# RWKV's chunk inverses per head on 64x64 quadrants instead of block-diagonal 128x128 matrices of two heads

## The chip, the core and the metric

One NeuronCore of a Trainium2 chip runs the whole program: TensorE (PE) for matmuls, VectorE (DVE), ScalarE (ACT) and GpSimd (POOL) for the elementwise work, SyncE (SP) and the others' queues for DMA. The metric is the device time of one execution in microseconds; three runs are given by their median, 3457.86 us (3451.37 to 3464.75).

## The reference, cut to what matters

Three blocks follow one another (an attention and retention block, a gated MLP and state space block, and a block with sparse attention and RWKV). The change is in the third block's RWKV part: 512 tokens, 8 heads of 64. For every head a state of 64x64 is carried from token to token:

```python
def _wkv7_step(state, inp):
    r, w, k, v, a, b = inp
    sa = jnp.einsum('bhvk,bhk->bhv', state, a)
    state = state * w[:, :, None, :] + sa[..., None] * b[:, :, None, :] + v[..., None] * k[:, :, None, :]
    return state, jnp.einsum('bhvk,bhk->bhv', state, r)

def rwkv7_time_mix(feats, w0, w2, a0, a2, g2, k_k, k_a, r_k, ln_w, ln_b):
    ...
    kk = heads(k * k_k)
    kk = kk / jnp.maximum(jnp.sqrt(jnp.sum(kk * kk, axis=-1, keepdims=True)), 1e-12)
    k = k * (1.0 + (a - 1.0) * k_a)
    ...
    xs = tuple(z.transpose(1, 0, 2, 3) for z in (rh, heads(decay), kh, vh, -kk, kk * ah))
    _, y = lax.scan(_wkv7_step, state0, xs)
    ...
```

Because each step adds a product of the state with `a` back into the state, a chunk of 64 tokens can be done at once only with the inverse of a triangular 64x64 matrix, (I - L)^-1, where L holds the products of the chunk's `a` and `b`, masked below the diagonal.

## The kernel before

The 8 heads are taken as 4 pairs. A pair fills the 128 partitions: head 0 in rows 0 to 63, head 1 in rows 64 to 127. Each pair has 8 chunks of 64 tokens, and all matrix work on chunks is in fp32.

`rwkv` runs, for each pair t: `raw` (three projections of the block's normed input, TensorE lines L250 to L252 with their weights split on ScalarE and VectorE), `features` (decays, normalised keys, the operands `ar`, `b`, `kt`), `prepare` (per chunk the matrix L and its inverse) and `steps` (the chunks in turn). They overlap by generators: while the 8 steps of pair t run, `prepare` of pair t + 1 advances by a stage per step, and after the fourth step `raw` and `features` of pair t + 2 are issued. During the last pair's steps, the sparse attention's preparation runs instead. The order in which the instructions of each engine stand is then fixed when the program is built, and projections of later blocks are spread between the small matmuls.

In `prepare` the chunks come in two groups u = 0, 1 of four. The steps that the change touches:

- L1705 and L1706 (GpSimd) copy `b` and `kt` into `bbd` and `kbd`, 128x128 matrices per chunk with head 0's 64x64 block in the upper left and head 1's in the lower right; the other blocks are zero from the start.
- L1710 (and L1764 for `kbd`) is the Gram product of this matrix with `ar`, 128 columns per chunk. L1712 (VectorE) masks it into `lt`, again block-diagonal, and L1717 and L1718 form the first `XT` (2x2 blocks and identity).
- `flip` (L1726) transposes `XT` per chunk on TensorE, L1727 copies it to `X`.
- `level(l)` for l = 1 to 5 doubles the diagonal blocks: GpSimd masks `lt` (L1736), L1741 multiplies it with half of X's columns, L1743 (ScalarE) copies the result into `ys`, L1747 multiplies that with half of XT's columns, L1749 (VectorE) adds it to XT, and a flip follows (except after the last).
- In `steps`, L1811 multiplies the inverse `xt` with a right hand side that L1805 copied; L1803, L1810, L1823 and L1826 are the other products of a step, one per head. L1816 and L1829 are VectorE links of the chain from step to step.

All per-chunk matrices of both heads are 128 wide, and half of each is zero:

```python
                    nc.tensor.matmul(g1[:, n].rearrange("p u l -> p (u l)"), bbd[u][:, n], rhs, start=True, stop=True)
                    nc.tensor.transpose(tt[:, n], XT[u][:, n], K.ident)
                        nc.tensor.matmul(y[u][:, n], ls[:, n], half(X[u], 0)[:, n], start=True, stop=True)
                        nc.tensor.matmul(yx[u][:, n], ys[u][:, n], half(XT[u], 1)[:, n], start=True, stop=True)
                nc.tensor.matmul(sa, xt[:, n], rs_, start=True, stop=True)
```

Of the kernel before, what the change touches and what calls it, by code (L numbers as in the profile page):

```python
# [7 lines left out]
def tw(w):  # L8
    """[K, N] -> [N/128, 128, K]: block n holds, for each row within a row block, its row blocks' 128 columns"""
    K, N = w.shape  # L10
    return np.ascontiguousarray(
        w.reshape(K // 128, 128, N // 128, 128).transpose(2, 1, 0, 3)).reshape(N // 128, 128, K)


def tn(w):
    """[K, m] -> [128, K/128 * m]"""
    K, m = w.shape
    return np.ascontiguousarray(w.reshape(K // 128, 128, m).transpose(1, 0, 2)).reshape(128, K // 128 * m)


def il(w, n=2):
    """block order a0 a1 .. b0 b1 .. -> a0 b0 a1 b1 .."""
# [4 lines left out]
class Vec:  # L27
    """per-feature vectors, packed as columns of [128, n]"""
# [14 lines left out]
    def dup(self, name, v):  # L43
        """a [64] vector on both halves"""
# [13 lines left out]
def shape_consts():  # L58
# [10 lines left out]
    half = 64  # L69
# [11 lines left out]
    m = np.zeros((128, 8, 128), f)  # L81
    m[:, 0, :64] = np.arange(64)[None, :] > h[:, None]
    m[:, 0, 64:] = np.arange(64)[None, :] >= h[:, None]
    b = i[:, None] // 64 == i[None, :] // 64
    for l in range(6):
        z = 1 << l
        s_, t_ = h[:, None], h[None, :]
        m[:, 1 + l] = b & (s_ // (2 * z) == t_ // (2 * z)) & (s_ // z % 2 == 0) & (t_ // z % 2 == 1)
    m[:, 7, 0] = i >= 31
# [13 lines left out]
def arrays1(I, vec):  # L103
    """layouts for the first block"""
# [92 lines left out]
class Ctx:  # L197
# [13 lines left out]
    def psum(self, mm, s=0, t=0, o=0):  # L211
        """the banks: for projections, scores, transposes, and sums over several steps"""
# [19 lines left out]
    def wunit(self, src, kc, m=P):  # L232
        """src: DRAM AP [128, kc*m]; gives hi, lo tiles [128, kc, m]."""
# [20 lines left out]
    def ahead(self, key, *args, **kw):  # L254
        """a block whose result is asked for later, by the same key"""
        self.early[key] = self.block(*args, **kw)

    def block(self, srcs, xs, halves, m=P, pss=None, first=True, last=True, key=None, unit=None):
        """srcs: list of (DRAM AP, kc); xs: list over all kc of (hi, lo) APs [128, T].
        halves: list of (start, size) of token columns. Returns psum APs."""  # L260
# [33 lines left out]
    def stacked(self, out, x, s):  # L294
        """rows 64 s .. of x: hi parts in the same rows of out, lo parts in the other half"""
# [5 lines left out]
    def twice(self, hi, lo, x, s):  # L301
        """hi and lo parts of rows 64 s .. of x, each on both halves"""
# [7 lines left out]
    def unstack(self, out, ps):  # L310
        """the two halves of a bank added"""
# [13 lines left out]
    def sq_acc(self, acc, h, first, scale=1.0):  # L325
        """acc += (h * scale)^2"""
# [9 lines left out]
    def rstd(self, acc, halves, eps, name, pool=None, factor=None):  # L336
        """rstd of the columns, times factor if there is one, on all partitions: exp(-ln(mean + eps) / 2)"""
# [31 lines left out]
    def swiglu(self, w_up, w_dn, zs, rs, halves, hid, done):  # L369
        """w_up: DRAM [44, 128, 1024] with blocks a0 b0 a1 b1 ..; w_dn: [8, 128, 22*128]."""  # L370
# [21 lines left out]
    def setup_consts(self, c):  # L392
        """c: DRAM [128, 7, 128]: identity, blocks of 1/64, a quarter of the upper triangle, last row,
        causal mask (0 / -1e30 above), 1/256, 1/512"""
# [23 lines left out]
    def bcast(self, ap):  # L418
        """DRAM AP read by all partitions"""
        return bass.AP(tensor=ap.tensor, offset=ap.offset, ap=[[0, P]] + [list(x) for x in ap.ap])  # L420

    def log1p(self, out, y, s, q):
        """ln(1 + y) for 0 <= y <= 1, as 2 atanh(y / (2 + y)); s and q are scratch"""
# [11 lines left out]
    def rstd_mm(self, sq, ones, eps, pool, name, psum=None):  # L435
        """exp(-ln(ones^T sq + eps) / 2), sq [128, <=512] fp32 (overwritten)"""
# [14 lines left out]
    def newton(self, r, ms, eps, u, spread=True):  # L451
        """one step for r ~ 1 / sqrt(ms + eps); u is scratch; spread: on three engines"""
# [11 lines left out]
    def head_sq(self, t, pool, bufs=2):  # L464
        """squares, and their hi and lo parts"""
# [8 lines left out]
    def head_fin(self, sq, halves, eps, pool, bufs=2, spread=False):  # L474
        """1 / sqrt of each head's mean"""
# [23 lines left out]
def act_tables(nc):  # L499
    """loads ScalarE's table sets where a function needs another one: the set that serves the most functions ahead"""  # L500
# [1499 lines left out]
```

## Time and profile before

| | |
|---|---|
| median of 3 runs | 3457.86 us (3451.37 to 3464.75) |
| span of the profiled execution (what the profile gives as its own time) | 3469.6 us |
| TensorE busy | 3344.1 us (96%), 17777 matmul passes |
| VectorE, ScalarE, GpSimd busy | 1955.4, 1416.7, 755.8 us |
| mean granted clock of TensorE | 0.981 |
| RWKV's chunk work | about 2576 to 2920 us |

Busy times are of one profiled execution, from its first to its last instruction; 11.7 us above the median run. A granted clock of 1.0 is 2.4 GHz, 0.5 is 1.2 GHz. Starts of matmuls are recorded, ends modelled, so the spacing of starts is the better measure of what a pass costs. An fp32 matmul shows as two passes, each with a weight load; a group such as "x16" on one row is sixteen passes. The forms are written as rows by columns of the array: 128*128 is the whole array, 64*64 a quadrant, and behind it the shape of the moving operand.

### The profile page before, as it was taken

Reading aid. Unit: us, or ns where it says so; the run is one execution under the profiler, and the core shown is the slowest. Engines: PE = TensorE matmul, PEld = TensorE weight load, DVE = VectorE, ACT = ScalarE, POOL = GpSimd, SP = SyncE. Lnnn points to the kernel's source line nnn. Section 1 sums busy time; section 2 is a strip of 40 time slices with the busy share of each in tenths; the row PEclk is TensorE's granted clock in tenths of the full one; section 3 lists DMA queues with packets and bytes.
Section 4 is the critical chain, followed back from the end, with each engine's and each line's share of the span. In section 5 each row is a group of like instructions: output and inputs, shape, how many; then the busy total and the mean of one; then the engine's idle time right before and its main releaser. Section 6 shows DMA issues by size and latency. Waiting matters only on the chain. (4 is left out here: it accounts for less than half of the span.)

```text
span 3469.6 us, 45531 instructions
## 1 busy us (share of the span) xinstructions
PE 3344.1 (96%) x17777; PEld 2764.7 (80%) x17777; DVE 1955.4 (56%) x3248; ACT 1416.7 (41%) x2474; POOL 755.8 (22%) x786
## 2 busy tenths in 40 slices
PE   8999999999999999999999999999989998999999
PEld 7999977878777888867777778888878776768887
DVE  4443366656654443278776664666366656766642
ACT  3222366643333222245554333444334434654431
POOL 2211133321112111112211321111234432421100
PEclk9999999999999999999999999999999988999999
DMA  3323222232133333333332323333330012123233
GB/s 121 89 91 90 87 81 74 74 104 92 59 95 97 95 94 93 96 92 94 92 100 85 114 89 92 94 95 96 113 95 26 23 47 80 41 60 97 94 101 94
DMA packets 89590, 298.63 MB, mean 86 GB/s; under 512 B 10711, under 2 KB 11351, under 8 KB 89120
## 3 DMA queue, kind: packets, MB, share of 16 engines
q1 hardware_dynamic: 76896, 260.70, 24.5%
q0 software_dynamic: 6416, 23.80, 2.4%
q10 hardware_dynamic: 6064, 11.23, 1.0%
q8 instruction: 139, 2.28, 0.3%
q14 instruction: 75, 0.61, 0.1%
HBM read 288.22 MB, written 7.47 MB: 85 GB/s over the span
## 5 line engine op out<-in xcount | busy, mean ns | idle before, releaser
L250 PE MATMUL mm<-zh,wh 128*128 128x512 f32 (+1 forms) x3296 | 1187.4, 360 | 20.1 <-ACT zh L291 8.7
L252 PE MATMUL mm<-zh,wl 128*128 128x512 f32 (+1 forms) x3296 | 1190.1, 361 | 3.3 <-DVE wl L244 3.2
L251 PE MATMUL mm<-zl,wh 128*128 128x512 f32 (+1 forms) x3296 | 1182.7, 359 | 4.2 <-DVE zl L292 4.2
L240 ACT ACTIVATE wh<-w 128x1024 fp32r<-128x1024 f32 (+2 forms) x523 | 523.7, 1001 | 1088.7 <-PE mm L251 771.1
L244 DVE TENSOR_TENSOR wl<-w,wh 128x1024 fp32r<-128x1024 f32 (+2 forms) x523 | 626.1, 1198 | 400.0 <-ACT wh L240 391.1
L250 PEld LDWEIGHTS mm<-zh,wh 128*128 128x128 f32 x3296 | 621.8, 189 | 117.3 <-issue 9.1
L251 PEld LDWEIGHTS mm<-zl,wh 128*128 128x128 f32 x3296 | 623.1, 189 | 103.6 <-DVE zl L292 5.1
L252 PEld LDWEIGHTS mm<-zh,wl 128*128 128x128 f32 x3296 | 622.8, 189 | 95.8 <-DVE wl L244 6.4
L250 PE MATMUL mm<-hh,wh 128*128 128x512 f32 (+1 forms) x880 | 308.7, 351 | 0.0
L251 PE MATMUL mm<-hl,wh 128*128 128x512 f32 (+1 forms) x880 | 308.5, 351 | 0.0
L252 PE MATMUL mm<-hh,wl 128*128 128x512 f32 (+1 forms) x880 | 307.9, 350 | 0.0
L252 PEld LDWEIGHTS mm<-hh,wl 128*128 128x128 f32 x880 | 165.7, 188 | 23.3
L251 PEld LDWEIGHTS mm<-hl,wh 128*128 128x128 f32 x880 | 165.7, 188 | 23.1
L250 PEld LDWEIGHTS mm<-hh,wh 128*128 128x128 f32 x880 | 165.7, 188 | 23.1
L382 POOL TENSOR_TENSOR ta<-ta,rs 128x264 f32<-128x264 f32 (+1 forms) x66 | 85.9, 1314 | 395.7 <-ACT ta L381 395.7
L334 POOL TENSOR_TENSOR acc<-acc,ta 128x512 f32<-128x512 f32 (+1 forms) x49 | 83.4, 1703 | 350.3 <-ACT ta L333 349.9
L1000 POOL TENSOR_TENSOR cv<-cv 128x512 f32<-128x512 f32 x44 | 57.5, 1306 | 436.3 <-DVE cv L981 398.8
L981 DVE SCALAR_TENSOR_TENSOR cv<-ta,vec,cv 128x510 f32<-128x510 f32 (+1 forms) x176 | 132.0, 753 | 3.1 <-ACT cv L978 0.3
L384 DVE TENSOR_TENSOR tb<-mm,ta 128x264 f32<-128x264 f32 (+1 forms) x66 | 32.8, 519 | 142.1 <-PE mm L252 138.3
L995 DVE TENSOR_TENSOR ta<-mm,rs 128x512 f32<-128x512 f32 x88 | 60.3, 687 | 59.6 <-PE mm L252 59.5
L380 DVE TENSOR_TENSOR ta<-mm,rs 128x264 f32<-128x264 f32 (+1 forms) x66 | 32.5, 518 | 107.8 <-PE mm L252 107.8
L282 ACT ACTIVATE hh<-cv 128x512 fp32r<-128x512 f32 x44 | 27.8, 633 | 144.1 <-POOL cv L1000 144.1
(596 smaller groups left out, 4829.1 us busy)
## 6 DMA issues: line engine op xcount, KB each, us to landing
w<-in_w_up_dram SPq DMA_DIRECT2D x176, 512.0 KB, 3.5
w<-in_w_in_dram SPq DMA_DIRECT2D x160, 512.0 KB, 3.5
w<-in_w_dn_dram SPq DMA_DIRECT2D x64, 512.0 KB, 3.5
w<-in_w_dn_dram SPq DMA_DIRECT2D x32, 384.0 KB, 3.1
w<-in_w_out_dram SPq DMA_DIRECT2D x16, 512.0 KB, 3.6
aB<-acum_d POOLq DMA_DIRECT2D x16, 512.0 KB, 6.0
w<-in_w_pb_dram SPq DMA_DIRECT2D x32, 256.0 KB, 3.0
negc<-negc_d POOLq DMA_DIRECT2D x8, 528.0 KB, 4.1
```

The lines of the kernel that those rows point to most:

```text
L240: nc.scalar.activation(h_, w_, AF.Copy)
L244: nc.vector.tensor_sub(l_, w_, h_.bitcast(F32))
L250: nc.tensor.matmul(ps, wh, xh, start=start, stop=False)
L251: nc.tensor.matmul(ps, wh, xl, start=False, stop=False)
L252: nc.tensor.matmul(ps, wl, xh, start=False, stop=stop)
L334: nc.gpsimd.tensor_tensor(acc, acc, q, op=ALU.add)
L380: nc.vector.tensor_mul(ta, a, rs[:, c])
L382: nc.gpsimd.tensor_tensor(ta, ta, rs[:, c], op=ALU.mult)
L384: nc.vector.tensor_mul(tb, b, ta)
L981: nc.vector.scalar_tensor_tensor(y[:, d:], x[:, :T - d], w(i), y[:, d:], op0=ALU.mult, op1=ALU.add)
L995: nc.vector.tensor_mul(x, p, rs)
L1000: nc.gpsimd.tensor_tensor(y[1], y[1], y[0], op=ALU.mult)
```

## The change

Nothing is block-diagonal any more. `lt`, `XT`, `X`, `ls` and `ys` hold a 64x64 matrix per head and chunk, head 0 in partitions 0 to 63 and head 1 in 64 to 127, and every product is made per head by `heads`: one matmul with operands and result in partitions 0 to 63, one in 64 to 127. `bbd` and `kbd` with their memsets and copies are gone, the Gram products take `b` and `kt` themselves. The flip is no transpose any more but a matmul of `XT` with a 64x64 identity. The masks shrink with them. In the changed file, comments and docstrings are removed too, and a few lines are added, so line numbers move by up to four: L1803 becomes L1805, L1811 becomes L1815, and all products of `heads` stand on one line, L1707.

```diff
-        bbd, kbd, lt = ([T(f"{n}{u}", (P, 4, P)) for u in range(2)] for n in ("bbd", "kbd", "lt"))
-        for x in (*bbd, *kbd, *lt):
-            nc.gpsimd.memset(x, 0.0)
+        lt = [T(f"lt{u}", (P, 4, 64)) for u in range(2)]
...
+            def heads(out, a, b):
+                for h in hv:
+                    nc.tensor.matmul(out[h], a[h], b[h], start=True, stop=True)
             X, XT = [], []
             for u in range(2):
-                n4 = slice(4 * u, 4 * u + 4)
-                for h in hv:
-                    nc.gpsimd.tensor_scalar(bbd[u][h, :, h], e8(b)[h, n4], 1.0, 1.0, op0=ALU.mult, op1=ALU.mult)
-                    nc.gpsimd.tensor_scalar(kbd[u][h, :, h], e8(kt)[h, n4], 1.0, 1.0, op0=ALU.mult, op1=ALU.mult)
                 g1 = K.ss([P, 4, 2, 64])
                 for n in range(4):
                     rhs = ar[:, 4 * u + n].rearrange("p u l -> p (u l)")
-                    nc.tensor.matmul(g1[:, n].rearrange("p u l -> p (u l)"), bbd[u][:, n], rhs, start=True, stop=True)
-                for h in hv:
-                    nc.vector.tensor_mul(lt[u][h, :, h], g1[h, :, 0], mb(h, 0))
+                    heads(g1[:, n].rearrange("p u l -> p (u l)"), tok(b, 4 * u + n), rhs)
+                nc.vector.tensor_mul(lt[u], g1[:, :, 0], mb(slice(0, P), 0))
...
-                X.append(T(f"x{u}").rearrange("p (n m) -> p n m", n=4))
-                XT.append(TB("xt", (P, 4, P), bufs=4))
+                X.append(T(f"x{u}", (P, 4, 64)))
+                XT.append(TB("xt", (P, 4, 64), bufs=4))
                 nc.vector.tensor_tensor(XT[u], lt[u], lv(0), op=ALU.mult)
-                nc.vector.tensor_tensor(XT[u], XT[u], K.ident.unsqueeze(1).to_broadcast([P, 4, P]), op=ALU.add)
+                nc.vector.tensor_tensor(XT[u], XT[u], id64.unsqueeze(1).to_broadcast([P, 4, 64]), op=ALU.add)
...
             def flip(u):
-                tt = K.st([P, 4, P])
+                tt = K.st([P, 4, 64])
                 for n in range(4):
-                    nc.tensor.transpose(tt[:, n], XT[u][:, n], K.ident)
+                    heads(tt[:, n], XT[u][:, n], id64)
                 nc.scalar.activation(X[u], tt, AF.Copy)
...
-                shp = [P, 4, 64 >> l, 1 << l]
+                shp = [P, 4, 32 >> l, 1 << l]
...
-                        nc.tensor.matmul(y[u][:, n], ls[:, n], half(X[u], 0)[:, n], start=True, stop=True)
+                        heads(y[u][:, n], ls[:, n], half(X[u], 0)[:, n])
...
-                        nc.tensor.matmul(yx[u][:, n], ys[u][:, n], half(XT[u], 1)[:, n], start=True, stop=True)
+                        heads(yx[u][:, n], ys[u][:, n], half(XT[u], 1)[:, n])
...
-                    nc.tensor.matmul(g2_[:, n].rearrange("p u l -> p (u l)"), kbd[u][:, n], rhs, start=True, stop=True)
+                    heads(g2_[:, n].rearrange("p u l -> p (u l)"), tok(kt, 4 * u + n), rhs)
...
-                nc.tensor.matmul(sa, xt[:, n], rs_, start=True, stop=True)
+                for s in range(2):
+                    h = slice(64 * s, 64 * s + 64)
+                    nc.tensor.matmul(sa[h], xt[h, n], rs_[h], start=True, stop=True)
```

How TensorE's order looks at the last level of one pair, while steps of the pair before run. In the kernel before, `t<-x,ls` is L1741's product of a group of four chunks (one row is four matmuls), `s<-xt,ys` is L1747's, `o<-` are products of a step, `mm<-` are projections:

```order
L1741 MATMUL t<-x_22849,ls 128x64 x4
L251 MATMUL mm<-zl_21349,wh 128x512
L252 MATMUL mm<-zh_21348,wl 128x512
L1741 MATMUL t<-x_22866,ls 128x64
L1811 MATMUL o<-rsb,xt 128x64
L1741 MATMUL t<-x_22866,ls 128x64 x3
L1747 MATMUL s<-xt,ys_23374 128x64 x4
L1747 MATMUL s<-xt,ys_23383 128x64 x4
```

The same place in the changed kernel:

```order
L1707 MATMUL t<-x_23102,ls 64x32 x8
L251 MATMUL mm<-zl_21349,wh 128x512
L1707 MATMUL t<-x_23118,ls 64x32 x8
L1707 MATMUL s<-xt,ys_23743 64x32 x8
L1827 MATMUL o<-lrb,h_22576 64x64
L1707 MATMUL s<-xt,ys_23756 64x32 x8
L1805 MATMUL o<-h_22576,ml 64x64 x2
```

Each group has eight matmuls on quadrants instead of four on the whole array, with half the moving columns. Projections still stand between some of the groups, and each of them is a change between the quadrants and the whole array that was none before.

GpSimd's order at the start of a pair's preparation. `lw` is the tile of `b`, `a` that of `kt`; before:

```order
L1684 TENSOR_TENSOR lw<-kk,a 128x512
L1681 TENSOR_TENSOR ar<-r,ec 128x8x64
L1685 TENSOR_TENSOR lw<-lw,en 128x512
L1705 TENSOR_SCALAR bbd_21524<-lw 64x4x64 x2
L1705 TENSOR_SCALAR bbd_21525<-lw 64x4x64 x2
L1692 TENSOR_TENSOR a<-k,en 128x512
L1706 TENSOR_SCALAR kbd_21526<-a 64x4x64 x2
L1706 TENSOR_SCALAR kbd_21527<-a 64x4x64 x2
L1736 TENSOR_TENSOR ls<-lt_21528,msk 128x512
```

And in the changed kernel:

```order
L1685 TENSOR_TENSOR lw<-kk,a 128x512
L1682 TENSOR_TENSOR ar<-r,ec 128x8x64
L1686 TENSOR_TENSOR lw<-lw,en 128x512
L1693 TENSOR_TENSOR a<-k,en 128x512
L1738 TENSOR_TENSOR ls<-lt_21527,msk 128x256
L1738 TENSOR_TENSOR ls<-lt_21528,msk 128x256
```

The eight copies are gone, the rest stands in the same order, and the masking of `lt` is half as wide.

## Rows read from the trace of the kernel before

**Rows 1.** Busy time by stretch: engine busy (instructions), PEclk is the granted clock, DMA share, GB/s.

```profile
2660.00:2720.00 60.00, 58.17 (x421) 45.90 (x421) 41.58 (x86) 26.01 (x60) 26.71 (x31) 1.00 0.09 27
2720.00:2780.00 60.00, 56.58 (x419) 46.87 (x418) 39.63 (x77) 25.85 (x58) 24.95 (x28) 1.00 0.06 16
...
2835.00:2866.00 31.00, 30.69 (x142) 25.09 (x142) 9.04 (x41) 6.94 (x19) 9.32 (x14) 0.51 0.07 21
```

**Rows 2.** Groups by line, TensorE, 2576 to 2925: count | busy us, mean ns | idle before.

```profile
L1747 PE MATMUL s<-xt,ys 128*128 128x64 f32 x320 | 43.9, 290 | 0.3 <-DVE fx L1663 0.2
L1741 PE MATMUL t<-x,ls 128*128 128x64 f32 x320 | 43.4, 284 | 1.4 <-ACT x L1727 0.9 <-issue 0.6
L1726 PE MATMUL t<-cst,xt 128*128 128x128 f32 x160 | 24.2, 285 | 1.3 <-DVE xt L1718 1.3
...
L1811 PE MATMUL o<-rsb,xt 128*128 128x64 f32 x64 | 14.0, 305 | 3.2 <-ACT rsb L1805 3.1
```

**Rows 3.** TensorE in time order: start us, us from first start to last end, count, [idle].

```profile
2661.48 1.00 PE L1741 MATMUL t<-x,ls 128*128 128x64 f32 x8
2662.42 0.27 PE L1823 MATMUL o<-lrb,h 64*64 64x64 f32 x1
2662.43 0.27 PE L1823 MATMUL o<-lrb,ssb 64*64 64x64 f32 x1
...
2662.68 0.50 PE L252 MATMUL mm<-zh,wl 128*128 128x512 f32 x1
2663.02 1.00 PE L1741 MATMUL t<-x,ls 128*128 128x64 f32 x8
```

**Rows 4.** The same view at 2820 us, two column-pair lines in a row.

```profile
2820.70 0.34 PE L1803 MATMUL o<-h,ml 128*64 128x64 f32 x4
2820.86 0.29 PE L1810 MATMUL o<-ml,h 128*64 128x64 f32 x4
2821.08 0.44 PE L1747 MATMUL s<-xt,ys 128*128 128x64 f32 x2
```

**Rows 5.** The same view at 2684 us, one run of flips.

```profile
2684.41 1.05 PE L1726 MATMUL t<-cst,xt 128*128 128x128 f32 x8
```

**Rows 6.** The same view at 1566 us, the longest run of column pairs.

```profile
1566.44 1.09 PE L1112 MATMUL o<-E,xdt 128*64 128x128 f32 x16
```

**Rows 7.** GpSimd in time order, the copies at the first two pairs.

```profile
2589.87 3.29 POOL L1705 TENSOR_SCALAR bbd<-lw 64x256 f32<-64x256 f32 x4
...
2646.92 2.43 POOL L1705 TENSOR_SCALAR bbd<-lw 64x256 f32<-64x256 f32 x3
```

**Rows 8.** Waits of TensorE, 2576 to 2925: us in total, times, longest.

```profile
PE s L1710 <- POOL bbd L1705: 7.3, 3, 3.7
PE o L1803 <- DVE h L1829: 5.2, 5, 2.4
PE o L1823 <- DVE h L1816: 4.9, 8, 1.2
```

**Rows 9.** TensorE in time order, the last pair's levels.

```profile
2834.02 1.08 PE L1741 MATMUL t<-x,ls 128*128 128x64 f32 x8 [0.88 <-ACT x L1727]
...
2838.26 3.68 PE L1747 MATMUL s<-xt,ys 128*128 128x64 f32 x16
...
2844.62 3.68 PE L1741 MATMUL t<-x,ls 128*128 128x64 f32 x16
2848.09 3.62 PE L1747 MATMUL s<-xt,ys 128*128 128x64 f32 x16
```

**Rows 10.** Groups by line, VectorE and ScalarE, 2576 to 2860.

```profile
L1749 DVE TENSOR_TENSOR xt<-s,xt 128x256 f32<-128x256 f32 x40 | 16.8, 420 | 42.5 <-PE s L1747 42.4
...
L1827 DVE TENSOR_TENSOR s<-o,s 64x128 f32<-64x128 f32 x21 | 5.9, 281 | 13.1 <-PE o L1826 12.9
...
L1743 ACT ACTIVATE ys<-t 128x256 f32<-128x256 f32 x40 | 15.1, 388 | 20.4 <-PE t L1741 20.2
```

More of the change, by code (lines that the diff above doesn't have):

```diff
@@ L80, in shape_consts @@
     h = i % 64
-    m = np.zeros((128, 8, 128), f)
+    m = np.zeros((128, 5, 128), f)
     m[:, 0, :64] = np.arange(64)[None, :] > h[:, None]
     m[:, 0, 64:] = np.arange(64)[None, :] >= h[:, None]
-    b = i[:, None] // 64 == i[None, :] // 64
     for l in range(6):
         z = 1 << l
-        s_, t_ = h[:, None], h[None, :]
-        m[:, 1 + l] = b & (s_ // (2 * z) == t_ // (2 * z)) & (s_ // z % 2 == 0) & (t_ // z % 2 == 1)
-    m[:, 7, 0] = i >= 31
+        s_, t_ = h[:, None], np.arange(64)[None, :]
+        m[:, 1 + l // 2, 64 * (l % 2):64 * (l % 2) + 64] = (
+            (s_ // (2 * z) == t_ // (2 * z)) & (s_ // z % 2 == 0) & (t_ // z % 2 == 1))
+    m[:, 4, 0] = i >= 31
     ch = np.ones((128, 512), f)
@@ L1365, in prepare @@
         late = T("late", (P, 1))
-        nc.scalar.dma_start(late, D["cmask"][:, 7, :1])
+        nc.scalar.dma_start(late, D["cmask"][:, 4, :1])
         gt = T("gt", (P, 4, 24))
@@ L1602, in rwkv @@
         TB = lambda name, shape=(P, 512), dt=F32, bufs=1: rp.tile(list(shape), dt, name=name, bufs=bufs)
-        msk, ch = T("msk", (P, 7, P)), T("chunk")
-        nc.scalar.dma_start(msk, D["cmask"][:, :7])
+        msk, ch = T("msk", (P, 4, P)), T("chunk")
+        nc.scalar.dma_start(msk, D["cmask"][:, :4])
+        id64 = T("id64", (P, 64))
+        for h in range(2):
+            nc.vector.tensor_copy(id64[64 * h:64 * h + 64], K.ident[64 * h:64 * h + 64, 64 * h:64 * h + 64])
         nc.scalar.dma_start(ch, D["chunk64"])
@@ L1698, in prepare @@
             mb = lambda h, i: m0[h, i:i + 1].to_broadcast([h.stop - h.start, 4, 64])
-            lv = lambda l: msk[:, 1 + l:2 + l].to_broadcast([P, 4, P])
+            lv = lambda l: msk[:, 1 + l // 2:2 + l // 2, 64 * (l % 2):64 * (l % 2) + 64].to_broadcast([P, 4, 64])
             hv = [slice(0, 64), slice(64, 128)]
+            tok = lambda x, n: x[:, 64 * n:64 * n + 64]
+            def heads(out, a, b):
+                for h in hv:
+                    nc.tensor.matmul(out[h], a[h], b[h], start=True, stop=True)
             X, XT = [], []
             for u in range(2):
-                n4 = slice(4 * u, 4 * u + 4)
-                for h in hv:
-                    nc.gpsimd.tensor_scalar(bbd[u][h, :, h], e8(b)[h, n4], 1.0, 1.0, op0=ALU.mult, op1=ALU.mult)
-                    nc.gpsimd.tensor_scalar(kbd[u][h, :, h], e8(kt)[h, n4], 1.0, 1.0, op0=ALU.mult, op1=ALU.mult)
                 g1 = K.ss([P, 4, 2, 64])
@@ L1731, in level @@
                 half = lambda x, i: x.rearrange("p n (b t j) -> p n b t j", t=2, j=1 << l)[:, :, :, i]
-                shp = [P, 4, 64 >> l, 1 << l]
+                shp = [P, 4, 32 >> l, 1 << l]
                 y, ys, yx = {}, {}, {}
                 for u in range(2):
-                    ls = T("ls", (P, 4, P), bufs=2)
+                    ls = T("ls", (P, 4, 64), bufs=2)
                     nc.gpsimd.tensor_tensor(ls, lt[u], lv(l), op=ALU.mult)
-                    ys[u] = T(f"ys{u}").rearrange("p (n m) -> p n m", n=4)
+                    ys[u] = T(f"ys{u}", (P, 4, 64))
                     nc.gpsimd.memset(half(ys[u], 1), 0.0)
```

## The prediction

> **What bounds the kernel now.** I read the table of stretches first, because the change touches only the time in which RWKV's chunk matrices are built (from about 2576 us, where the first pair's features start, to about 2860 us, after the last pair's fifth level). The reader is to see that TensorE is busy nearly all of it: 58.17 of 60 us from 2660 to 2720, at the full clock, against 41.58 for VectorE and less for the others [rows 1]. So a microsecond of TensorE work removed here is nearly a microsecond of the kernel, as long as nothing else becomes late. The second thing to see is the stretch 2835 to 2866: busy 30.69 of 31 us, but at a granted clock of 0.51, that is 1.2 instead of 2.4 GHz. Next come the groups by line: the two products of a level (L1741 and L1747) have 320 passes each, the flips (L1726) 160, the step's product with the inverse (L1811) 64 [rows 2]. An fp32 matmul shows as two passes, a transpose as one.
>
> **The change, part by part.** Counts are for the whole stage: 4 pairs of heads, 5 levels, 8 chunks, in two groups of four chunks.
>
> *Passes removed.* Eight passes of L1741 take 1.00 us with a last one of about 0.27 [rows 3], and sixteen in a row start 3.47 us apart from the next line where the clock is halved [rows 9], so a pass costs 0.104 to 0.112 us at full clock; I take 0.112 in steady running, 0.90 for a group of eight. That is independent of the 64 columns that move. Eight flips take 1.05 us, (1.05 - 0.27) / 7 = 0.111 a pass [rows 5], 0.45 for a group of four. Before: 80 groups of eight at 0.90 are 72.0, 40 groups of flips at 0.45 are 18.0, 64 passes of L1811 at 0.11 are 7.0; together 97.0 us.
>
> *Passes added.* Each of these becomes two matmuls on the quadrants 0-63 and 64-127, and the flips become real fp32 matmuls against a 64x64 identity, with two passes where a transpose has one. In the trace such pairs exist: L1823's two matmuls, one per half, start at 2662.42 and 2662.43, so the two quadrants run side by side [rows 3]. How fast pairs of passes follow one another must be bounded. The fastest row is L1803 followed by L1810, column pairs of 64 by 64: they start at 2820.70 and 2820.86, and L1810's two pairs of passes take 0.29 us where one pass takes 0.22 [rows 4], so a pair of passes costs 0.06 to 0.08 us. The slowest is L1112: 16 passes in 1.09 us, (1.09 - 0.27) / 15 = 0.055 a pass, 0.109 a pair, but there 128 columns move [rows 6]. The new products move 32 or 64 columns, so the nearest row is the first and I take 0.06. A group of four chunks is then 8 x 0.06 = 0.48: 120 groups (two products and a flip, 40 each) are 57.6, the step's product 32 x 0.12 = 3.8; together 61.4. The Gram products (L1710, L1764) move 128 columns and keep 0.109 a pair, as a pass before: nothing. Passes together: 61.4 - 97.0 = -35.6.
>
> *Changes of mode, added.* The quadrant form stands between projections and transposes that use the whole array, and a change costs time. L1741's eight passes start at 2661.48 and would end their slots 0.90 later; L252 would take 0.23 more (its mates start that far apart); so without L1823 in between the next L1741 could start at 2662.61. It starts at 2663.02 [rows 3]. Of these 0.41 us the two pairs of passes are 0.12, which leaves 0.29 for two changes, 0.145 each. I counted the changes of form (whole array, two column halves, two row halves, quadrants) along TensorE's order, from the first L1652 to the last L1823: 225 before, 354 now. 129 x 0.145 = +18.7. The Trainium skill, TensorEngine Tiling (Array Packing), section Key Properties, says that changing the tiling mode, not just the tile, drains TensorE. The trace agrees, with its 0.145 us; the page has no price, and by its section Theoretical Speedup alone (up to 2x a side) there would be a gain and no such cost.
>
> *The halved clock.* Between 2838 and 2852 about six groups of products run at 1.2 GHz (sixteen passes 3.47 us instead of 1.80) [rows 9]; their saving of 0.42 a group counts double there: -2.5.
>
> *GpSimd's copies, removed.* The Gram product waits for two of the copies that build the block-diagonal operand: four of them, behind L1685 in GpSimd's order, take 3.29 us, three 2.43 at the next pair [rows 7]; two are 1.65 and 1.62. Now b itself is the operand and the product can start when L1685 ends. TensorE waited 7.3 us there in three waits [rows 8], so of that 3.3 go: -3.3. What is late next is the chain of features before it, which stays. At the last two pairs TensorE had projections to do and nothing is won.
>
> *Smaller elementwise work.* Operands shrink from 128x512 to 128x256, and L1749 and L1743 from 128x256 to 128x128 [rows 10]. None of these engines bounds the stage, so by itself it counts nothing; it shortens the hand-overs below.
>
> *Hand-overs, exposed.* While the first group's product goes to ScalarE or VectorE and back, TensorE does the second group's, 0.90 us so far, 0.48 now. A hand-over is some 0.22 for the last pass, the copy or add (0.28 by L1827's 64x128, 0.39 by L1743's 128x256, which is the size of the flip's copy now) [rows 10] and, by estimate, 0.1 for signals: 0.60, 0.60 and 0.71. Short of cover by 0.12, 0.12 and 0.23, that is 0.47 a level, 9.4 us over 20 levels, nothing where a projection or a step stands between, and below nothing only if waits for VectorE shorten. The order has something between in about half of the places: +5. Behind a waiting product stand the step's matmuls and the projections, in order, and the step's ScalarE and VectorE work waits for those.
>
> *Clock, one level more.* The last pair's levels have no projections between them, and the clock fell there after a wait of 0.88 us for L1727 [rows 9]. With shorter groups it may fall a level earlier: about the 3 us of a level's TensorE work, which I weigh at +2.
>
> Sum: -35.6 + 18.7 - 2.5 - 3.3 + 5 + 2 = -15.7 us on the profiled execution, whose span is 3469.6 us, 11.7 above the median of the three runs. The saving is the same in both, so 3457.9 - 15.7 = 3442.
>
> **Rivals.**
>
> *A. As summed,* 3442, own range 3430 to 3453 (a change of mode at 0.11 to 0.19 us, hand-overs 0 to 9.4).
>
> *B. The passes saved turn into waits:* with 9.4 us of hand-overs and 5 more for steps whose VectorE links come in queue order, -15.7 + 9.4 = about 3451 to 3456, no change. For it: TensorE already waits 5.2 us for L1829 [rows 8]. Against: VectorE and GpSimd have less to do in every level.
>
> *C. The halved stretch goes as well:* 31 us at 0.51 done at full clock are some 15 less, and half of the waits for VectorE's links (5.2 for L1829, 4.9 for L1816) [rows 8], 5 less: 3422. For it: fewer passes of 64 columns bring projections closer together. Against: in that stretch there are none.
>
> *D. Slower: short passes can't be issued at 0.03 us each.* The longest run in the trace faster than 0.055 a pass is eight passes (L1803, L1810) [rows 4]; the sixteen of L1112 stand at 0.055 [rows 6], and a group now has sixteen, with three groups in a row at places. If 0.055 is what a long run gets, a product's group takes 0.88 as before (-1.6 in all), a flip 0.88 instead of 0.45 (+17.2), L1811 stays; with the changes of mode 18.7 and the copies -3.3 the sum is +31: 3489. It decides from about 0.042 us a pass, where the passes saved (0.23 a product's group, lost again by the flips) no longer pay for the changes of mode. Against it: between groups there are projections, two instructions in 0.23 us, in which a queue can fill. The Trainium skill, TensorE: Matmul & The Clock Gate, section "Wait — 56ns, not 53.3ns?", says that with hardware decode off the sequencer spends about 62 ns per matmul, which binds when the array's work is shorter. By that a group of sixteen would take 0.99 us and the sum, an estimate from that page, would be near +46; the eight passes of rows 4 went faster, so at least a short run is not bound so.
>
> *E. Slower: the clock falls in the levels of the middle pairs too.* The levels take about 35 us of each of the stretches 2660 to 2720 and 2720 to 2780, which ran at full clock. Were both at half, each would take some 25 to 30 us more, less the 15.7: 3482 or more. For it: the fall at 2835 came in a stretch of level work with few projections [rows 1, 9]. Against: the same level work with projections between held the full clock for 60 us [rows 1].
>
> That the change doesn't do what it says is no rival: the order shows the quadrant matmuls.
>
> **How the numbers follow.** A 0.48, B 0.12, C 0.20, D 0.14, E 0.06. Half a per cent, about what a measurement of this kernel can tell from no change, is 17.3 us: faster means under 3440.6, slower over 3475.2. A straddles the lower edge (0.20 under it, 0.28 over); with C that is 0.40 faster; A's rest and nearly all of B are 0.39 same; D, E and a hundredth of B 0.21 slower. The range runs from C with a bit more to D: 3412 to 3489.
>
> **What would show it.** Right: L1707's pairs start side by side, eight pairs of passes in about 0.5 us; TensorE's busy time in the stage falls by about 15 to 20 us; the wait of L1707 for GpSimd is 3 to 4 us instead of 7.3; the first pass after a change of form starts about 0.15 us late. Wrong: groups of sixteen passes that take 0.8 us or more (D); waits of 0.2 to 0.5 us before most products, on ScalarE or VectorE, summing to over 12 us (B); a granted clock of 0.5 for more than some 50 us of the stage (E) or for none of it (C).

## The result, and the profile after

The changed kernel takes 3428.2 us (median of four runs, 3426.9 to 3430.7) against 3461.3 (3451.4 to 3465.9) for the kernel before in the same job: ratio 0.990, 95% interval 0.987 to 0.992, 33 us. The forecast was 3442, faster by 16. The time lies in its range and on the side given the largest chance, but 14 us under the point and 2 us under the likeliest case's own range: it is nearer to rival C's 3422 (chance 0.20) than to the point, and the range holds it because C is in it.

The kernel before doesn't always take the same time. The 17 executions of it beside the experiments below fall into two groups: eight of 3449 to 3457 us at a mean granted clock of 0.985 to 0.988, nine of 3465 to 3471 at 0.980 to 0.982. The changed kernel's five are at 0.988. Time multiplied by mean granted clock, which counts every microsecond at 1.2 GHz as half lost, the most that it can lose, is 3408 and 3405 us on the mean of the two groups and 3388 for the changed kernel. So at equal clock the change is worth 17 to 20 us, some 18 on the mean, and the rest of the difference, 5 us against the one group and 23 against the other, goes with the clock. Both profiles of the kernel before that are shown here ran at a low clock (0.981 and 0.983).

The table of stretches of the kernel after (columns as in [rows 1]) shows the same picture at first sight, TensorE busy nearly all the time. The line to look at is the last one: where the kernel before had a clock of 0.51 [rows 1] there is 0.87.

```profile
2660.00:2720.00 60.00, 57.73 (x633) 39.81 (x627) 41.40 (x90) 24.06 (x56) 16.05 (x19) 1.00 0.09 30
2720.00:2780.00 60.00, 57.62 (x701) 39.54 (x702) 36.33 (x85) 22.32 (x58) 15.68 (x23) 0.94 0.10 32
2780.00:2835.00 55.00, 54.63 (x765) 39.35 (x762) 30.30 (x89) 23.78 (x61) 19.30 (x30) 1.00 0.20 61
2835.00:2866.00 31.00, 24.50 (x194) 18.90 (x190) 22.34 (x73) 11.39 (x32) 3.56 (x2) 0.87 0.24 77
```

Stretches of fixed times hold different work in the two kernels. A better ruler runs from event to event: from the first pair's matmul with w2a (L1652 before) to attention's first matmul with q (L1535 before). This stage is one row for each profiled execution, and each kernel was profiled twice (the second times as experiments, below). The kernel before, first and second profile:

```profile
2573.30:2944.50 371.20, 343.60 (x2153) 270.35 (x2153) 236.30 (x499) 147.86 (x318) 138.08 (x154) 0.91 0.14 43
```

```profile
2564.70:2937.80 373.10, 345.10 (x2153) 271.42 (x2153) 235.34 (x498) 147.75 (x318) 139.30 (x154) 0.90 0.13 43
```

The changed kernel, first and second profile:

```profile
2572.30:2903.60 331.30, 308.74 (x3464) 221.07 (x3464) 214.40 (x491) 135.00 (x318) 95.80 (x122) 0.96 0.15 49
```

```profile
2573.80:2909.90 336.10, 313.38 (x3465) 224.07 (x3465) 214.42 (x491) 135.09 (x318) 95.85 (x122) 0.95 0.15 48
```

The reader is to see three things. The stage is 38.5 us shorter on the mean (372.2 to 333.7), about what the runs show; what lies outside it differs by 10 us between the two profiles of the kernel before (3098 and 3089 us) and is 3094 and 3095 after, so the rest of the 44.5 us between the first two spans is scatter. TensorE's idle time, length less busy, went from 27.6 and 28.0 to 22.6 and 22.7. And the granted clock rose from 0.91 and 0.90 to 0.96 and 0.95: added up, the stretches at 1.2 GHz between 2560 and 2930 are 68 and 72 us before, 24 and 34 after.

The passes, in TensorE's groups by line (2565 to 2895) and in order of time, the counterparts of [rows 2, 3]:

```profile
L1707 PE MATMUL t<-id,xt 64*64 64x64 f32 x640 | 25.8, 225 | 3.5 <-DVE xt L1720 3.4
L1707 PE MATMUL t<-x,ls 64*64 64x32 f32 x640 | 25.7, 220 | 0.2 <-issue 0.2
L1707 PE MATMUL s<-xt,ys 64*64 64x32 f32 x640 | 25.6, 220 | 0.0
```

```profile
2662.81 0.47 PE L252 MATMUL mm<-zh,wl 128*128 128x512 f32 x1
2663.21 0.66 PE L1707 MATMUL t<-x,ls 64*64 64x32 f32 x16
2663.80 0.50 PE L250 MATMUL mm<-zh,wh 128*128 128x512 f32 x1
2664.23 0.45 PE L1830 MATMUL o<-h,h 128*64 128x64 f32 x4
...
2665.17 0.40 PE L250 MATMUL mm<-zh,wh 128*128 128x512 f32 x1
2665.49 0.66 PE L1707 MATMUL t<-x,ls 64*64 64x32 f32 x16
2665.98 0.63 PE L1707 MATMUL s<-xt,ys 64*64 64x32 f32 x16
```

Twice the instructions, and less time: two groups in a row start 0.49 us apart (2665.49 and 2665.98), where [rows 3] had 0.9 a group. Between L252 and L250 the group takes 0.59 us, 0.10 more, the price of leaving the quadrant form; L1707 starts 0.40 after L252, where without a change it would be 0.23.

TensorE's waits after (2576 to 2925), beside [rows 8]:

```profile
PE o L1830 <- DVE h L1820: 4.0, 3, 2.4
PE t L1707 <- DVE xt L1720: 3.4, 1, 3.4
PE s L1707 <- POOL lw L1686: 3.2, 2, 1.8
PE o L1805 <- DVE h L1833: 3.1, 4, 1.7
PE o L1827 <- DVE h L1820: 2.9, 6, 1.1
```

The Gram product's wait for GpSimd is 3.2 us instead of 7.3, and a wait of 3.4 stands right behind it, the first flip for VectorE's XT (L1720), where the kernel before waited 1.3 [rows 2]: half of what the copies gave up came back at the next link.

### The profile page after: what moved, and what is told of

It reads as the page before. It is cut to its first block, busy times and chain, and to the rows that moved or that the text cites. A ratio compares the mean times of both kernels' runs of the same rounds, so it can differ in the third digit from the quotient of the medians.

```text
span 3425.1 us, 48109 instructions
## 1 busy us (share of the span) xinstructions
PE 3307.4 (97%) x19089; PEld 2713.7 (79%) x19089; DVE 1933.8 (56%) x3242; ACT 1404.5 (41%) x2474; POOL 713.6 (21%) x748
## 5 line engine op out<-in xcount | busy, mean ns | idle before, releaser
L250 PE MATMUL mm<-zh,wh 128*128 128x512 f32 (+1 forms) x3296 | 1186.2, 360 | 19.7 <-ACT zh L291 8.7
L252 PE MATMUL mm<-zh,wl 128*128 128x512 f32 (+1 forms) x3296 | 1187.7, 361 | 3.9 <-DVE wl L244 3.8
L250 PEld LDWEIGHTS mm<-zh,wh 128*128 128x128 f32 x3296 | 620.8, 188 | 116.6 <-ACT zh L291 8.7
L252 PEld LDWEIGHTS mm<-zh,wl 128*128 128x128 f32 x3296 | 621.0, 188 | 99.1 <-DVE wl L244 7.3
L250 PE MATMUL mm<-hh,wh 128*128 128x512 f32 (+1 forms) x880 | 308.5, 351 | 0.0
L252 PE MATMUL mm<-hh,wl 128*128 128x512 f32 (+1 forms) x880 | 307.6, 350 | 0.0
L252 PEld LDWEIGHTS mm<-hh,wl 128*128 128x128 f32 x880 | 165.6, 188 | 23.2
L250 PEld LDWEIGHTS mm<-hh,wh 128*128 128x128 f32 x880 | 165.5, 188 | 23.2
```

The source lines that it names most:

```text
L250: nc.tensor.matmul(ps, wh, xh, start=start, stop=False)
L252: nc.tensor.matmul(ps, wl, xh, start=False, stop=stop)
```

## Experiments

Theory: the passes bring what the forecast said, the changes of form cost something near their 18.7 us, and the clock in the last pair's levels is what the forecast missed. Rivals: the changes of form cost nothing in their places; the Gram products and the copies bring the gain; the quadrants gain by shortness alone and not by running side by side; and the places where the clock falls are chance.

**Which part: the Gram products alone, and the levels alone.** The kernel before, with the Gram products per head and without the copies:

```
-  nc.gpsimd.tensor_scalar(bbd[u][h, :, h], e8(b)[h, n4], ...)    # and kbd
-  nc.tensor.matmul(g1[:, n]..., bbd[u][:, n], rhs, ...)
+  heads(g1[:, n]..., tok(b, 4 * u + n), rhs)                      # L1764 likewise
```

> The kernel before with one part of the change alone: the Gram products are made per head on quadrants from b and kt, the block-diagonal copies and their memsets are gone; levels, flips and the step's product stay on the whole array. Theory S (the sum, with the clock on top): copies -3.3, 30 more changes of form at 0.145 are +4.4, so -4 to +4 us against the kernel before; the stretch at half clock in the last pair's levels stays, the mean granted clock stays near 0.98. Rival R (a change of form costs next to nothing in place, and the clock has no part; the 33 us are passes and copies alone): -3 to -8 us.

Measured: 3456.8 us (3451.7 to 3469.3), ratio 0.999, interval 0.9975 to 1.0005: no change that can be measured. Its profile (3458.7 us; the twelve executions lie between 3451.7 and 3469.3) holds two parts, though. The matmuls with g2 (L1845 before), one at each pair's end, stand 79.2 us apart from the first to the second pair (75.5 and 76.3 in the two profiles before), and 62.4 from the second to the third, while the last pair's matrices are built (75.4 in both profiles before). This is the row of the second piece, with the same levels as before and no halved clock, which theory S did not expect:

```profile
2800.00:2862.40 62.40, 61.28 (x488) 47.76 (x487) 34.29 (x98) 27.38 (x62) 25.40 (x30) 1.00 0.17 53
```

The same piece of the kernel before (second profile) and of the changed kernel (first), for comparison:

```profile
2788.70:2864.10 75.40, 73.22 (x456) 58.88 (x455) 34.56 (x97) 27.15 (x62) 26.26 (x30) 0.80 0.14 44
```

```profile
2774.30:2831.70 57.40, 57.03 (x789) 40.51 (x788) 32.97 (x96) 24.12 (x62) 20.03 (x30) 1.00 0.22 68
```

The clock (0.80 to 1.00) gave 13 us in this piece, the levels on quadrants, at the same clock, another 5. In the Gram kernel some 6 of the 13 were lost ahead of it, of which 30 more changes of form (225 to 255) are, by estimate, 3 to 4. All this is read from one execution; whether the order of the Gram products kept the clock up in it is not shown (see the repeated profiles below). The reverse, the changed kernel with block-diagonal copies for the Gram products again:

> The changed kernel with the other part alone: levels, flips and the step's product per head on quadrants, but the Gram products on the whole array from block-diagonal copies as before. Theory S: about -25 to -32 us against the kernel before, with the mean granted clock near 0.988 and no halved stretch of 30 us in the last pair's levels; the two parts add up to the whole within 5 us. Rival R: -25 to -30 too, but with the clock as low as before.

Measured: 3432.9 us (3429.7 to 3435.4), ratio 0.991, interval 0.990 to 0.993, which overlaps that of the whole change. The levels carry nearly all of the gain; that the Gram products bring nothing measurable fits their added changes of form and the wait at the next link, but those two were not tested apart.

**Side by side, or only shorter?** The changed kernel with head 0's four chunks ahead of head 1's, in the products and the flips:

```
-  for n in range(4):
-      heads(tt[:, n], XT[u][:, n], id64)
+  for h in hv:
+      for n in range(4):
+          nc.tensor.matmul(tt[h, n], XT[u][h, n], id64[h], ...)
```

> The changed kernel with the order of the matmuls in a group turned: first the four chunks of head 0, then the four of head 1, instead of the heads in turn; the same matmuls on the same quadrants. If the quadrants run side by side only for neighbours in the order, a group of sixteen passes takes 16 x 0.056 = 0.9 instead of 0.46 us, 120 groups give about +50 us against the changed kernel (about 3480). If TensorE looks far enough ahead to fill both quadrants, or if the saving doesn't come from running side by side, it stays within 5 us of the changed kernel.

Measured: 3458.5 us (3452.5 to 3467.2), ratio 0.9988, interval 0.9973 to 1.0003: 30 us over the changed kernel, the whole gain. Its TensorE in order of time shows a group of sixteen passes (L1713 is L1707 there):

```profile
2725.10 0.40 PE L252 MATMUL mm<-zh,wl 128*128 128x512 f32 x1
2725.42 0.96 PE L1713 MATMUL t<-id,xt 64*64 64x64 f32 x16
2726.32 0.50 PE L250 MATMUL mm<-zh,wh 128*128 128x512 f32 x1
```

That is a group of flips; in the changed kernel one takes 0.68. Two groups of products in a row between the same neighbours, first in the serial and then in the changed kernel:

```profile
2684.70 1.43 PE L1713 MATMUL t<-x,ls 64*64 64x32 f32 x32
```

```profile
2675.29 1.12 PE L1707 MATMUL t<-x,ls 64*64 64x32 f32 x32
```

So a group costs 0.16 to 0.28 us more, by estimate 20 to 30 us over 120 groups. The two heads overlap only where one ends and the other begins. The rise is short of the forecast 50 us, but far over the 5 us of the other theory. The clock has a part in it: the stretches at 1.2 GHz in the stage are 58 us here, 24 and 34 in the changed kernel, and at equal clock (time multiplied by clock, 3404 against 3388) some 16 of the 30 us are left. So the form helps when neighbours in the order lie on different quadrants; but passes one behind the other on one quadrant (about 0.06 us each) are still cheaper than those of the whole array (0.11).

**The price of a change of form.** Into the changed kernel's product groups go 160 one-column bf16 matmuls, one after the second and one after the third chunk, whose result nothing reads: on the whole array in one kernel (single matmuls; the expectation's "pairs" is a slip), as quadrant pairs in the other.

```
+  def probe(o): nc.tensor.matmul(o[:, 256:257], K.ident_bf, K.ident_bf[:, :1], ...)                   # e4
+  def probe(o):
+      for h in hv: nc.tensor.matmul(o[h, 256:257], K.ident_bf[h, h], K.ident_bf[h, :1], ...)          # e5
```

> The changed kernel with 160 pairs of one-column bf16 matmuls on the whole array put inside its product groups (two groups of L1741 and L1747 each get one after the second and the third chunk); they write a column that nothing reads. Changes of form along TensorE's order go from 353 to 673. Theory S (each change of form costs about 0.145 us wherever it stands): with some 5 us for the probes themselves, about 52 us over the changed kernel, 3480. Rival (a change costs only where TensorE would have waited anyway, so the 18.7 us of the sum were never paid): 3430 to 3440. The pair e5_quad has the same probes without the changes; the difference of the two is the price, 329 changes: 48 us by S, under 10 by the rival.

> The same probes as in e4_mode in the same places, but as pairs of quadrant matmuls (0-63 and 64-127), so that the form does not change: 344 changes of form. All theories: 160 x two pairs of short passes at 0.03 to 0.06 us, some 5 to 10 us over the changed kernel's 3428: 3432 to 3440.

Measured: 3497.9 us (3484.3 to 3507.8; ratio 1.0105, interval 1.0075 to 1.0135) with changes, 3426.6 (3424.5 to 3428.2; ratio 0.990, interval 0.988 to 0.992) without. The rival is out: with 329 more changes the kernel takes 71 us longer, and the probes themselves cost nothing that shows. But 71 is more than theory S's 48, and the traces tell why in part. TensorE in order of time, first with changes, then without:

```profile
2628.44 0.18 PE L1710 MATMUL s<-identb 128*128 128x1 bf16 x1
2628.55 0.30 PE L1707 MATMUL s<-xt,ys 64*64 64x32 f32 x4
2628.78 0.18 PE L1710 MATMUL s<-identb 128*128 128x1 bf16 x1
2628.89 0.31 PE L1707 MATMUL s<-xt,ys 64*64 64x32 f32 x4
```

```profile
2722.27 0.28 PE L1707 MATMUL s<-xt,ys 64*64 64x32 f32 x4
2722.39 0.17 PE L1711 MATMUL s<-identb 64*64 64x1 bf16 x2
2722.42 0.28 PE L1707 MATMUL s<-xt,ys 64*64 64x32 f32 x4
```

Four passes and a probe take 0.34 us (2628.55 to 2628.89) with two changes, 0.15 (2722.27 to 2722.42) without: 0.19 for two, not quite 0.10 each, where the forecast had 0.145. Over 329 that is some 31 us, if all of it is on the path. The clock is the other source: the stretches at 1.2 GHz in the stage are 102 us with changes and 20 without, and half of the difference is 41. The two do not simply add up to the 71: the profiled execution with changes is the shortest of its four (3484.3 us), and the two profiled spans are only 60 us apart (3482.2 and 3422.3), so the clock or the changes take less there than these figures. At equal clock (time multiplied by clock, 3406 against 3389 over all executions) 17 us are left, 0.05 a change, as a lower bound. The price of a change of form in these places lies between that and 0.10.

**Two groups of four chunks made one of eight.** The same products in the same form, one hand-over where there were two, 331 changes of form instead of 353:

```
-  for u in range(2):
-      y[u] = K.st(shp)
-      for n in range(4): heads(y[u][:, n], ls[:, n], half(X[u], 0)[:, n])
+  y = K.st(shp)
+  for n in range(8): heads(y[:, n], ls[:, n], half(X, 0)[:, n])
```

> The changed kernel with the two groups of four chunks made one of eight (they now fit one PSUM bank): half as many copies, adds and masks, each twice as long, and 331 instead of 354 changes of form, but no second group to cover a hand-over. Theory that the second group's product covers the hand-overs (0.6 to 0.7 us each, 60 of them): +10 to +30 us against the changed kernel, with waits of TensorE for ScalarE and VectorE before most products. Rival, that projections and steps between them cover these: -3 us or a little more from the fewer changes and operations.

Measured: 3445.5 us (3437.4 to 3449.0), ratio 0.994, interval 0.992 to 0.996: 17 us over the changed kernel. Its table of stretches, the stage and a part of it:

```profile
2572.30:2927.10 354.80, 326.40 (x3465) 233.78 (x3465) 214.04 (x463) 129.73 (x278) 88.88 (x83) 0.90 0.14 46
2819.70:2850.40 30.70, 28.69 (x313) 22.24 (x312) 11.23 (x46) 5.73 (x18) 7.39 (x12) 0.50 0.18 57
```

The stage is 21 us longer than in the changed kernel (354.8 against 333.7). TensorE's idle time explains 5.7 of it (28.4 against 22.7). A stretch of 30.7 us at 0.50 in the last pair's levels, as in the kernel before, explains up to 15. So the time is the theory's, but not its reason: TensorE's products waited for ScalarE's copies at most 1.2 us in all, and at equal clock (3390 against 3388) next to nothing is lost. The projections stand elsewhere too, 45 passes between the second and the third matmul with g2 where the changed kernel has 66, so the grouping is not the only difference in the order.

**Chance, or the order of work?** Both kernels once more, unchanged:

> The kernel before, unchanged, profiled a second time, to see how far the places and lengths of its stretches at 1.2 GHz differ between executions. If the forecast's reading holds (the fall near 2835 belongs to this order of work), the new profile shows a halved stretch of about 31 us between the last pair's second and fifth level again. Rival (the stretch is one of several places where the clock can fall, and varies from execution to execution): it is missing or elsewhere, and the span is shorter by about half its length.

> The changed kernel, unchanged, profiled a second time. Theory (the places where the clock falls belong to the order of work): again no stretch at 1.2 GHz of over 10 us before 2850, and one of about 14 us near 2858; 3426 to 3431. Rival (they vary from execution to execution): a stretch of 20 to 30 us somewhere in the last pair's levels.

Measured: 3464.3 and 3433.0 us (the latter 2 over its expectation). The kernel before has the halved stretch again, at the same place (it begins 1.6 us behind the same wait for L1727's flips, here 0.97 us), and just as long; this is its row, first of the two:

```profile
2828.90:2859.60 30.70, 30.39 (x139) 24.78 (x139) 9.04 (x41) 6.64 (x18) 9.40 (x14) 0.50 0.08 21
2890.30:2907.40 17.10, 12.32 (x57) 8.55 (x57) 10.76 (x24) 7.47 (x16) 5.39 (x5) 0.50 0.12 32
```

The changed kernel has none in the last pair's levels and one of 13.7 us in its last steps, as expected; a stretch of 17.1 at 2596, in the first pair, was not expected. For these two profiles of each kernel the falls in the last pair stay in their places, those of the first pair vary. That the place belongs to the order of work is not settled by this. Eight of the 17 other executions of the kernel before were 15 us shorter at a higher clock, which is what the rival expected of executions without the stretch: by their mean clock they ran some 92 us at 1.2 GHz in all, where the two profiles have 131 and 120. None of the eight was profiled, so where they kept the clock is not shown. From the second pair's matmul with g2 to the third's it is 75.4 us in both profiles before (2795.5 to 2870.9, 2788.7 to 2864.1) and 57.4 in both after. That is 18 of the 38.5 us, in the piece in which the last pair's matrices are built.

**What is the halved stretch worth?** The kernel before, with 80 matmuls of 256 columns in the last pair's levels, four behind each product group, which nothing reads:

```
+  def fill(o):
+      if t == 3:
+          for _ in range(4):
+              nc.tensor.matmul(o[:, 256:512], z[:, :128], z[:, :256], start=True, stop=True)
```

> The kernel before with work added: in the last pair's levels, after each product group, four matmuls of 256 columns that nothing reads (80 of them at some 0.11 to 0.13 us, 9 to 10 us of TensorE work at full clock). Theory (the 31 us at 1.2 GHz in the last pair's levels are a matter of what stands between the short products, and cost some 12 to 15 us): the stretch runs at full clock in spite of the added work, and the kernel comes out at 3450 to 3460, 0 to 10 us faster than before. Rival (the halved stretch is tied to something else, or costs nothing on the path): 5 to 15 us slower, 3467 to 3477, and the stretch near 2835 to 2866 still shows 0.5.

Measured: 3467.4 us (3463.2 to 3473.1), ratio 1.0021, interval 1.0007 to 1.0035: slightly slower, so the theory's time is wrong and the rival's (3467 to 3477) came out, though not its halved stretch. The table of stretches shows that the sum has two parts, the same place and the next fall:

```profile
2828.90:2859.60 30.70, 30.47 (x246) 25.75 (x246) 12.93 (x51) 10.00 (x26) 13.04 (x19) 1.00 0.18 58
2880.40:2911.10 30.70, 25.15 (x127) 19.30 (x127) 16.85 (x51) 11.53 (x32) 4.17 (x4) 0.50 0.13 35
```

The levels ran at full clock, and the 75.4 us from the second pair's matmul with g2 to the third's became 73.1 in spite of about 9.6 us of added matmuls (80 at 0.12). So the halved stretch cost some 12 us there. But in the steps behind it the clock then stayed low for 30.7 us instead of 17.1. What the stretch is worth in its place is shown. That the filling kept the clock up is not: the profiled execution had the highest clock of its twelve (0.986, of 0.983 to 0.986), and the kernel before runs without so much low clock half the time. Nor is it shown that a kernel is faster for such filling.

**Filling the steps too.** Two kernels were to hold the clock in the last pair's steps, one made of the changed kernel, one of the kernel with the fill above. After each of a step's three links, chunks 4 to 7, they add

```
+  for s in (0, 1, 0, 1):
+      nc.tensor.matmul(w[64 * s:64 * s + 64, 256:512], K.ident[:, 64 * s:64 * s + 64], m2, ...)
```

> The changed kernel with work added: in the last pair's steps, chunks 4 to 7, two extra pairs of 256-column fp32 matmuls that nothing reads after each of the step's three links (11 places, some 0.45 us each, 5 us of TensorE work). In the changed kernel the clock falls at 2858 for 13.7 us, right after waits of 1.7 and 1.1 us in these steps. Theory (the fall follows such waits, and the extra work stands inside them): the 13.7 us at 1.2 GHz are gone; 3421 to 3430, 0 to 7 us faster than the changed kernel. Rival (the clock falls anyway, and the extra work is paid): 3430 to 3435.

> The kernel before with the extra work of both kinds, in the last pair's levels (as in e6_fill) and in its steps (as in e8_after_fill), 15 us of TensorE work that nothing reads. Theory (of the changed kernel's 33 us some 22 are the clock in the last pair, 48 us at 1.2 GHz in the kernel before): no stretch at 1.2 GHz of over 10 us is left between 2825 and 2925, and the kernel takes 3445 to 3455, faster than before by 5 to 15 us in spite of the added work, and faster than e6_fill by 12 to 20. Rival (the clock falls somewhere else, or is worth less than its length says): 3460 to 3475.

Measured: 3458.2 us (3454.0 to 3464.3) and 3489.9 (3486.9 to 3494.6), 30 and 22 over what each was made from; every number expected was missed. The added work was not what I had put it at. TensorE of the first, in order of time:

```profile
2848.60 0.48 PE L1812 MATMUL o<-h,ml 128*64 128x64 f32 x4 [0.38 <-DVE h L1843]
2848.84 0.45 PE L1820 MATMUL o<-ml,h 128*64 128x64 f32 x4
2849.39 1.97 PE L1804 MATMUL o<-msk,cst 128*64 128x256 f32 x8
2851.29 0.48 PE L1823 MATMUL o<-rsb,xt 64*64 64x64 f32 x4
```

One place takes 1.97 us and not 0.45, at 1.2 GHz (at 2.4 GHz its eight passes start 0.11 apart, so about 0.9), and it stands in the chain of the steps, ahead of the next link (L1823), rather than in its waits: the fill writes the tile that holds the links' results. The steps became longer, TensorE then waited 10.2 us once for attention's first operand (L1462), and the clock fell all the same, in the first kernel already at 2824.8 for 27.3 us, before the first added matmul. The projections had moved as well: 43 passes between the second and the third matmul with g2 instead of 66. So how the 30 us divide is open, and the two kernels say nothing about the worth of the clock.

## Why the prediction was right, and where its sum was not

*Passes.* Right: a group of four chunks was to take 0.48 us and starts 0.49 before the next. The side-by-side running on which this rests is shown by the serial order, which costs nearly the whole gain at equal clock (16 of 18 us).

*Rival D, short passes.* Refuted in its own terms: 32 passes in a row take 1.12 us in the merged kernel's order of time, (1.12 - 0.22) / 31 = 0.029 a pass, where the rival needed 0.055.

```profile
2817.51 1.12 PE L1707 MATMUL t<-x,ls 64*64 64x32 f32 x32 [0.37 <-ACT h L1770]
```

The Trainium skill, TensorE: Matmul & The Clock Gate, section "Wait — 56ns, not 53.3ns?", has some 62 ns a matmul where the hardware doesn't decode; the trace shows half of that even in long runs, so that case doesn't hold here.

*Changes of form.* The mechanism is right, 129 more of them, and not free, as the probes show. Where a group stands between two projections the rows after give 0.17 for the change in and 0.10 for the change out, 0.135 each; the probes' rows give 0.10, their times at equal clock at least 0.05. So the forecast's 0.145 (18.7 us) is at the upper end; at 0.10 the term would be 12.9. The Trainium skill, TensorEngine Tiling (Array Packing), section Key Properties, says that a change of the mode drains TensorE: the trace agrees that a change takes time, with 0.19 us for a pair of them.

*GpSimd's copies.* 3.3 us forecast, 4.1 in the wait's own row. It was named as late next: the chain of features stays. That the wait at the flips would grow from 1.3 to 3.4 us was missed, and alone this part brings nothing measurable.

*Hand-overs.* Forecast +5, with the copies +1.7 us of waiting. TensorE's idle time in the stage fell by 5.1 instead. The sign was wrong. The smaller copies (L1745 280 ns, from 388 [rows 10]) shorten the hand-over as the groups shorten the cover; that this is the reason was not tested.

```profile
L1745 ACT ACTIVATE ys<-t 128x128 f32<-128x128 f32 x40 | 10.9, 280 | 15.7 <-PE t L1707 15.1
```

*The clock.* This is the step that failed: "-2.5" for passes saved in the halved stretch and "+2" for a fall one level earlier, half a microsecond together. Instead the stretch of 30.7 us is gone in both profiles of the changed kernel, as rival C had it, at a chance of 0.20. The filled kernel puts its worth at 12 us, the Gram kernel at 13; all stretches together, 68 and 72 us to 24 and 34, are worth at most half of their difference, 20 us. The rest of the sum came out: without the two clock terms it is -15.2, against some 18 us at equal clock. With 12 to 20 for the clock and 6.8 for the waits (-5.1 instead of +1.7), the 22.8 us that the stage gained beyond the forecast are accounted for within a few. That holds for the profiled executions, which ran at a low clock. Against the eight executions of the kernel before at 0.985 to 0.988 the gain is 25 us, with some 5 for the clock. So the forecast also had the wrong picture in taking the halved stretch of one profile as a fixed part of the kernel before.

The argument against C ("in that stretch there are none", projections) fails twice. Its reading is wrong: from 2855.30 on the stretch holds 15 passes of projections. And its condition doesn't decide: the piece between the two matmuls with g2 holds the same 16 passes of L250 on the whole array in the profiles of the kernel before, the Gram kernel and the changed one, and the clock fell in the first alone.

```profile
2855.30 0.79 PE L250 MATMUL mm<-zh,wh 128*128 128x512 f32 x1
```

What tips the clock in the last pair's levels is open. The serial and the mode kernels fell there too (23.9 us from 2831.8, 37.5 from 2839.0), with no wait of TensorE over 0.25 us in the 38 us before, so it isn't a wait alone. The changed kernel doesn't fall there in its profiles, nor do its two halves; the Gram products alone have the very levels of the kernel before, so shorter levels aren't needed for it either. What is shown is that the stretch costs 12 to 13 us where it stands, and that the changed kernel's executions all ran at a high clock and those of the kernel before in about half of the cases. That the order of work alone decides it is not shown.

The measured 33 us carry an interval of 26 to 44; the stage's 38.5, from profiles at a low clock before, lie within it.

## What to carry to other kernels

Two small matmuls on different quadrants are worth ordering next to one another, pass by pass; head after head gives the gain away. Count the changes of form that such a split adds to TensorE's order, and price them at 0.10 to 0.15 us where TensorE has no slack, with a clock that may fall as well. Where a stretch at 1.2 GHz lies in the stage that is changed, look first at the clocks of several executions, for one profile doesn't tell whether it is always there. Then price both ends, that it stays and that it goes, before choosing a point: here that was more than half of the error.

## What the runs showed of the hardware

A change of form costs about the same at either clock. At 1.2 GHz four passes and a probe take 0.47 us with two changes (2608.65 to 2609.12) and 0.27 without (2597.57 to 2597.84, the only such place in the kernel with quadrant probes). The two changes are then 0.20, against 0.19 at 2.4 GHz.

```profile
2608.65 0.42 PE L1707 MATMUL s<-xt,ys 64*64 64x32 f32 x4
2609.01 0.19 PE L1710 MATMUL s<-identb 128*128 128x1 bf16 x1
2609.12 0.42 PE L1707 MATMUL s<-xt,ys 64*64 64x32 f32 x4
```

```profile
2597.57 0.41 PE L1707 MATMUL t<-x,ls 64*64 64x32 f32 x4
2597.78 0.20 PE L1711 MATMUL t<-identb 64*64 64x1 bf16 x2
2597.84 0.40 PE L1707 MATMUL t<-x,ls 64*64 64x32 f32 x4
```

Work that nothing reads can cost nothing (320 quadrant matmuls of one column, 3426.6 against 3428.2 us) or six times what was expected of it (44 matmuls in the steps, 30 us for 5), the second where it stood in a chain and the order around it changed too. And the clock can differ between executions of one and the same kernel: 0.980 to 0.988 over 17 of the kernel before, with times that differ by 15 us and, multiplied by the clock, by 3.
